# Low halves of split weights: a transfer that adds, in place of a subtraction on VectorE

## The chip, the cores and the metric

The kernel runs on one core of a Trainium2 chip. Its time is the device time of one execution in microseconds; the runs of the kernel before took 1648.26 to 1648.99 us, median 1648.5 us. Four engines compute beside each other, each with its own instruction queue worked off in order: PE (TensorE, matmuls), ACT (ScalarE), DVE (VectorE) and POOL (GpSimd). SP (SyncE) only issues transfers here.

## The reference

Two transformer blocks are computed one after the other, in fp32, for one sequence of 512 tokens with 1024 channels. The first has a gated convolution, block attention over 8 heads, cross-attention to 256 memory tokens, a gated merge and a feed-forward part of width 2816. The second has a pooling mixer, a spatial gating unit, a feed-forward part of the same width, and a gated addition. Most of the work is products with weight matrices, 151 MB in all, each weight used once:

```
proj = rmsnorm(x, g_mix) @ w_in
x = x + merged @ w_o
a, b = split(rmsnorm(x, g_ffn) @ w_up, 2)
x = x + (silu(causal_dwconv3(a)) * b) @ w_down
```

## The kernel before

All weights lie in one stream of 288 chunks, in the order in which they are used, each of 128 partitions x 1024 fp32 values (512 KB). The class `Weights` (lines 52 to 109) brings them in. `load` (line 67) issues one transfer for each chunk from SP into a raw tile `wraw`, of which there are three buffers. `make` (line 79) splits a chunk in two: ACT writes the high part `whi`, the weight rounded to the short matmul format fp32r (line 96), and DVE writes the low part `wlo`, the weight minus the high part (line 97). `whi` and `wlo` have three buffers each. The last 8 chunks are kept in tiles of their own.

`take` (line 101) hands out the next 128 or 512 columns. With the first columns of chunk c it has loads up to chunk c+2 and splits up to chunk c+1 issued. Activations are split in the same way, and every product is the sum of three matmuls, high x high, high x low and low x high:

```
mm(ps, lhsT=wh, rhs=ah, start=(k == 0), stop=False)
mm(ps, lhsT=wh, rhs=al, start=False, stop=False)
mm(ps, lhsT=wl, rhs=ah, start=False, stop=(k == n - 1))
```

These are lines 238 to 240, for products that come out with channels on partitions (`gemm_t`); lines 250 to 252 do the same for products with tokens on partitions (`gemm_n`, four tiles of 128 tokens that take turns). Both take 24 matmuls of 512 columns for one chunk. The first 8 chunks belong to the memory's keys and values, chunks 8 to 11 to the memory queries, chunks 12 to 15 to the attention queries, two steps k of the product for each chunk.

The order of instructions on each engine comes from a planner, which works with its own costs, apart from two stretches. From the start to line 459 (the products of the chunks up to 11) SP, ACT and DVE work in the order in which the program is written; PE's order is planned. From line 962 on ACT and DVE do so again.

POOL does little: it clears some tiles (lines 555, 558, 807), masks the spatial weights (line 779), scales the four `v` tiles of the gating unit (line 849), and adds squares for the last norm (line 307).

Of the kernel before, what the change touches and what calls it, by code (L numbers as in the profile page):

```python
# [7 lines left out]
F32 = mybir.dt.float32  # L8
# [3 lines left out]
AF = mybir.ActivationFunctionType  # L12
ALU = mybir.AluOpType
# [11 lines left out]
NCHUNK = 288  # L25
# [3 lines left out]


FILL = (4, 8)

ORDER = (2, 3, 1, 0)

# [17 lines left out]
class Weights:  # L52
# [26 lines left out]
    def make(self, upto, parts=1):  # L79

        while self.made < min(upto, NCHUNK):
            c = self.made
            nc = self.nc
            self.load(c + 1)
            raw = self.raw.pop(c)
            first, pool = self.stay
            if c < first:
                hi = self.pool.tile([P, CW], F32R, tag="whi", name=f"whi{c}", bufs=3)
                lo = self.pool.tile([P, CW], F32R, tag="wlo", name=f"wlo{c}", bufs=3)
            else:  # L90
                hi = pool.tile([P, CW], F32R, tag=f"whi{c}", name=f"whi{c}")
                lo = pool.tile([P, CW], F32R, tag=f"wlo{c}", name=f"wlo{c}")
            w = CW // parts
            for q in range(parts):
                s = slice(q * w, (q + 1) * w)
                nc.scalar.activation(hi[:, s], raw[:, s], AF.Copy)  # L96
                nc.vector.tensor_tensor(lo[:, s], raw[:, s], hi[:, s].bitcast(F32), ALU.subtract)  # L97
            self.chunks[c] = (hi, lo)
            self.made += 1

# [11 lines left out]
def build(ctx: ExitStack, tc: tile.TileContext, a: dict, out: bass.AP, dbg=None):  # L112
# [317 lines left out]
    def transpose_km():  # L430
        for g in range(2):
            pt = bank(ps_t, "pt", "kmt")
            for hh in range(2):
                for i in range(2):
                    c = (2 * g + hh) * P
                    nc.tensor.transpose(pt[:, hh * M + i * P: hh * M + (i + 1) * P], km_raw[i][:, c:c + P], ident)
            split(*kmT[g], pt, V("memk_gain"))


    for k in range(KT):  # L440
        if k == FILL[0]:
            transpose_km()
# [42 lines left out]
    def qkv_steps():  # L485
        for name, col, raws in (("q", 1536, q_raw), ("k", 2048, k_raw)):
            ps = [bank() for _ in range(4)]
            yield from gemm_n_steps(ps, h, "w_in", col)
            normed_rows(list(zip(raws, ps)), 8, name, rx)
        ps = [bank() for _ in range(4)]  # L490
        yield from gemm_n_steps(ps, h, "w_in", 2560)
        for i in range(4):
            src = ps[i].rearrange("p (g s d) -> p g s d", s=2, d=64)
            dst = vs[i].rearrange("p (g s o d) -> p g s o d", s=2, o=2, d=64)
            for s_ in range(2):
                split(dst[:, :, s_, s_, :], dst[:, :, s_, 1 - s_, :], src[:, :, s_, :], rx[:, i:i + 1])
# [36 lines left out]
    filler = qkv_steps()  # L533
    for _ in range(FILL[1]):
        next(filler)
# [607 lines left out]
```

## Time and profile before

| | before |
|---|---|
| median of 3 runs | 1648.5 us |
| profiled execution, its own time | 1648.37 us |
| its span, first to last instruction | 1646.7 us |
| mean granted TensorE clock | 0.998 of 2.4 GHz |
| PE, DVE, ACT, POOL busy | 99%, 57%, 39%, 2% of the span |
| DMA queue q1 (SP's transfers) | 31.4% of 16 engines' time |

A row of the timeline gives the start and the duration of an instruction in us, then engine, line of the kernel, operation, and the tile that it writes and those that it reads. Matmuls overlap: each is shown with some 0.39 us while the next starts 0.23 us after it, so rates are read from the starts. Idle time in brackets is that of the engine before the instruction, with what ended it.

### The profile page before, as it was taken

The page shows a single profiled execution, that of the slowest core. Times are in us where ns is not written, and L with a number is a line of the kernel's source. Part 1 is how long each engine was busy: PE and PEld are TensorE (multiplying, and loading weights), DVE is VectorE, ACT ScalarE, POOL GpSimd, SP SyncE. Part 2 cuts the span into 40 slices and gives each one's busy share as a digit, 9 for nine tenths or more (in the row PEclk, how much of TensorE's full clock was granted, in tenths as well). Part 3 has the DMA queues.
Part 4 walks back from the last instruction along what each step waited for, and adds up shares of the span by engine and source line. Part 5 has one row for each costly group of instructions (what it writes and reads, how often), then busy time and mean ns, then how long its engine had stood idle before and what let it go on. Part 6 is the DMA issues. An engine that isn't in the chain of part 4 may idle for free.

```text
span 1646.7 us, 18824 instructions
## 1 busy us (share of the span) xinstructions
PE 1632.1 (99%) x7495; PEld 1345.8 (82%) x7495; DVE 941.4 (57%) x1373; ACT 645.6 (39%) x926; POOL 24.8 (2%) x34
## 2 busy tenths in 40 slices
PE   8999999999999999999999999999999999999997
PEld 6788777888888888888888888888888888888896
DVE  6676785445556655653333943554567777753355
ACT  6555554223334333332224332332344444432242
POOL 0000000000000000000000300000000000000001
PEclk9999999999999999999999999999999999999999
DMA  8322222234333333332333232323332333323231
GB/s 319 108 77 65 64 57 82 93 102 143 101 96 97 95 98 96 96 102 90 102 117 100 91 103 90 92 88 103 92 114 92 100 97 96 102 90 103 90 115 52
DMA packets 47688, 165.01 MB, mean 100 GB/s; under 512 B 5361, under 2 KB 7025, under 8 KB 47601
## 3 DMA queue, kind: packets, MB, share of 16 engines
q1 hardware_dynamic: 47024, 163.04, 31.4%
q8 instruction: 58, 0.95, 0.2%
q10 hardware_dynamic: 576, 0.79, 0.1%
q14 instruction: 30, 0.24, 0.0%
HBM read 161.71 MB, written 2.10 MB: 99 GB/s over the span
## 4 chain that ended last, share of the span: by engine, by line
PE 96%; DVE 1%; DMA 1%; ACT 1%; issue 0%; ACTq 0%; DVEq 0%
PE acc L238 27%; PE acc L239 27%; PE acc L240 27%; PE acc L252 3%; PE acc L250 2%; PE acc L251 2%; DMA wraw<-in_weights 1%; PE pat L611 1%; PE acc L960 0%; PE acc L958 0%; PE acc L959 0%; PE sg L859 0%; PE oa L626 0%; PE oa L627 0%; PE sa L585 0%; ACT whi L96 0%
## 5 line engine op out<-in xcount | busy, mean ns | idle before, releaser
L96 ACT ACTIVATE whi<-wraw 128x1024 fp32r<-128x1024 f32 (+1 forms) x289 | 305.4, 1057 | 577.8 <-PE acc L239 353.6
L97 DVE TENSOR_TENSOR wlo<-wraw,whi 128x1024 fp32r<-128x1024 f32 (+1 forms) x289 | 353.3, 1222 | 221.0 <-ACT whi L96 219.5
L238 PE MATMUL acc<-h0h,whi 128*128 128x512 f32 x156 | 62.1, 398 | 0.0
L238 PE MATMUL acc<-h7h,whi 128*128 128x512 f32 x156 | 61.3, 393 | 0.0
L238 PE MATMUL acc<-h6h,whi 128*128 128x512 f32 x156 | 61.1, 392 | 0.0
L238 PE MATMUL acc<-h5h,whi 128*128 128x512 f32 x156 | 61.1, 392 | 0.0
L238 PE MATMUL acc<-h2h,whi 128*128 128x512 f32 x156 | 61.1, 391 | 0.0
L239 PE MATMUL acc<-h0l,whi 128*128 128x512 f32 x156 | 61.1, 391 | 0.0
L238 PE MATMUL acc<-h3h,whi 128*128 128x512 f32 x156 | 61.0, 391 | 0.0
L238 PE MATMUL acc<-h1h,whi 128*128 128x512 f32 x156 | 61.0, 391 | 0.0
L238 PE MATMUL acc<-h4h,whi 128*128 128x512 f32 x156 | 61.0, 391 | 0.0
L240 PE MATMUL acc<-h2h,wlo 128*128 128x512 f32 x156 | 60.9, 391 | 0.0
L239 PE MATMUL acc<-h7l,whi 128*128 128x512 f32 x156 | 60.9, 390 | 0.0
L239 PE MATMUL acc<-h2l,whi 128*128 128x512 f32 x156 | 60.9, 390 | 0.0
L240 PE MATMUL acc<-h5h,wlo 128*128 128x512 f32 x156 | 60.9, 390 | 0.0
L239 PE MATMUL acc<-h4l,whi 128*128 128x512 f32 x156 | 60.9, 390 | 0.0
L240 PE MATMUL acc<-h0h,wlo 128*128 128x512 f32 x156 | 60.9, 390 | 0.0
L239 PE MATMUL acc<-h5l,whi 128*128 128x512 f32 x156 | 60.9, 390 | 0.0
L239 PE MATMUL acc<-h1l,whi 128*128 128x512 f32 x156 | 60.8, 390 | 0.0
L240 PE MATMUL acc<-h6h,wlo 128*128 128x512 f32 x156 | 60.8, 390 | 0.0
L239 PE MATMUL acc<-h6l,whi 128*128 128x512 f32 x156 | 60.8, 390 | 0.0
L240 PE MATMUL acc<-h7h,wlo 128*128 128x512 f32 x156 | 60.8, 390 | 0.0
(1327 smaller groups left out, 4008.2 us busy)
## 6 DMA issues: line engine op xcount, KB each, us to landing
wraw<-in_weights SPq DMA_DIRECT2D x287, 512.0 KB, 3.5
xs<-in_xT SPq DMA_DIRECT2D x4, 512.0 KB, 6.2
x<-in_x SPq DMA_DIRECT2D x4, 512.0 KB, 9.3
x<-in_xT SPq DMA_DIRECT2D x8, 256.0 KB, 5.7
out<-o SPq DMA_DIRECT2D x5, 256.0 KB, 2.1
mem<-in_mem SPq DMA_DIRECT2D x2, 512.0 KB, 7.6
wraw<-in_weights SPq DMA_DIRECT2D x2, 256.0 KB, 4.6
memT<-in_memT SPq DMA_DIRECT2D x1, 512.0 KB, 7.8
```

The source lines that it names most:

```text
L96: nc.scalar.activation(hi[:, s], raw[:, s], AF.Copy)
L97: nc.vector.tensor_tensor(lo[:, s], raw[:, s], hi[:, s].bitcast(F32), ALU.subtract)
L238: mm(ps, lhsT=wh, rhs=ah, start=(k == 0), stop=False)
L239: mm(ps, lhsT=wh, rhs=al, start=False, stop=False)
L240: mm(ps, lhsT=wl, rhs=ah, start=False, stop=(k == n - 1))
L250: mm(ps, lhsT=ah[:, t], rhs=wh, start=(k == 0), stop=False)
L251: mm(ps, lhsT=ah[:, t], rhs=wl, start=False, stop=False)
L252: mm(ps, lhsT=al[:, t], rhs=wh, start=False, stop=(k == n - 1))
L611: nc.tensor.transpose(pt[:, i * P:(i + 1) * P], probs[s_][i][:, c0:c0 + P], ident)
```

## The change

For chunks 12 to 279 the subtraction on DVE is dropped. ACT writes the low tile with the negated weight, rounded in the same way as the high part, so with the negative of the high part; then a transfer issued by POOL adds the raw tile to it inside the low tile. Both tiles lie in the core's own memory (SBUF). The transfer has to wait for ACT's second pass, and PE's matmuls with the low part, and the next load into the raw tile's buffer, have to wait for the transfer. Chunks 0 to 11 and 280 to 287 are made as before.

```diff
+ADDED = range(12, NCHUNK - 8)
...
                 nc.scalar.activation(hi[:, s], raw[:, s], AF.Copy)
-                nc.vector.tensor_tensor(lo[:, s], raw[:, s], hi[:, s].bitcast(F32), ALU.subtract)
+                if c in ADDED:
+
+                    nc.scalar.activation(lo[:, s], raw[:, s], AF.Copy, scale=-1.0)
+                    nc.gpsimd.dma_start(lo[:, s], raw[:, s], accum_op=ALU.add)
+                else:
+                    nc.vector.tensor_tensor(lo[:, s], raw[:, s], hi[:, s].bitcast(F32), ALU.subtract)
```

## Rows read from the trace of the kernel before

**Rows 1.** Busy time by engine, page part 1: us, share of the span, instructions.

```profile
PE 1632.1 (99%) x7495; PEld 1345.8 (82%) x7495; DVE 941.4 (57%) x1373; ACT 645.6 (39%) x926; POOL 24.8 (2%) x34
```

**Rows 2.** Stretches of 50 us: busy us (instructions) by engine, clock, DMA share, GB/s.

```profile
0.00:50.00 50.00, 45.78 (x189) 33.68 (x189) 31.67 (x60) 30.73 (x46) 1.09 (x8) 1.00 0.77 278
50.00:100.00 50.00, 49.93 (x237) 38.88 (x236) 36.49 (x80) 28.71 (x54) 2.38 (x6) 1.00 0.32 97
...
750.00:800.00 50.00, 50.00 (x222) 41.38 (x222) 17.01 (x18) 13.18 (x15) 0.00 (x0) 1.00 0.34 103
...
900.00:950.00 50.00, 50.00 (x222) 41.42 (x221) 47.88 (x74) 18.43 (x25) 14.58 (x10) 1.00 0.33 105
...
1250.00:1300.00 50.00, 50.00 (x222) 41.42 (x221) 36.47 (x47) 22.46 (x28) 0.00 (x0) 1.00 0.31 97
...
1600.00:1650.00 50.00, 36.57 (x241) 33.39 (x239) 27.67 (x78) 14.08 (x34) 5.28 (x7) 0.92 0.12 43
```

**Rows 3.** Timeline of PE, first feed-forward part: start us, us, what, idle time before.

```profile
604.77 0.39 PE L238 MATMUL acc<-h0h,whi 128*128 128x512 f32 x1
...
610.21 0.39 PE L238 MATMUL acc<-h0h,whi 128*128 128x512 f32 x1
```

**Rows 4.** Groups by line, 277-1577 us: busy us, mean ns | idle before.

```profile
L97 DVE TENSOR_TENSOR wlo<-wraw,whi 128x1024 fp32r<-128x1024 f32 x237 | 290.8, 1227 | 199.1 <-ACT whi L96 198.2
L96 ACT ACTIVATE whi<-wraw 128x1024 fp32r<-128x1024 f32 x238 | 252.4, 1061 | 548.0 <-PE acc L239 345.7 <-issue 171.6 <-PE acc L252 19.0
```

**Rows 5.** Timeline of ACT, the stretch of rows 3.

```profile
604.74 1.06 ACT L96 ACTIVATE whi<-wraw 128x1024 fp32r<-128x1024 f32 x1 [3.06 <-PE acc L239]
605.71 0.80 ACT L636 ACTIVATE ca<-ta,vec 128x512 f32<-128x512 f32 x1
```

**Rows 6.** Timelines of POOL, ACT, DVE and PE, 903 to 930 us.

```profile
903.91 6.90 POOL L849 TENSOR_SCALAR sv<-sv,svy 128x1024 f32<-128x1024 f32 x2 [49.79 <-issue]
...
910.85 7.07 POOL L849 TENSOR_SCALAR sv<-sv,svy 128x1024 f32<-128x1024 f32 x2
...
929.04 0.12 POOL L807 MEMSET z<- 128x32 f32 x1 [8.59 <-DVE pl L820]
...
906.72 1.05 ACT L96 ACTIVATE whi<-wraw 128x1024 fp32r<-128x1024 f32 x1
...
908.09 2.06 DVE L97 TENSOR_TENSOR wlo<-wraw,whi 128x1024 fp32r<-128x1024 f32 x1
...
916.51 0.39 PE L240 MATMUL acc<-pd4h,wlo 128*128 128x512 f32 x1
```

**Rows 7.** DMA queue; line 75's issues and landings; SP's waits (us, times, longest).

```profile
q1 hardware_dynamic: 47024, 163.04, 31.4%
...
L75 SPq DMA_DIRECT2D wraw<-in_weights x289: 327/328/486, 1.2 to 1590.2; - x145
...
DMA to landing us min/median/max: 3.3/3.5/8.8
...
SPq L75 <- DVE wlo L97: 1339.8, 261, 10.7
```

**Rows 8.** Timelines of ACT, then PE, 48 to 60 us.

```profile
51.48 1.05 ACT L96 ACTIVATE whi<-wraw 128x1024 fp32r<-128x1024 f32 x1
...
53.47 1.05 ACT L96 ACTIVATE whi<-wraw 128x1024 fp32r<-128x1024 f32 x1
55.06 1.06 ACT L96 ACTIVATE whi<-wraw 128x1024 fp32r<-128x1024 f32 x1 [0.55 <-PE acc L252]
...
49.21 1.07 PE L250 MATMUL acc<-whi,h6h 128*128 128x512 f32 x4
...
55.09 0.39 PE L251 MATMUL acc<-wlo,h0h 128*128 128x512 f32 x1
...
56.45 0.39 PE L251 MATMUL acc<-wlo,h2h 128*128 128x512 f32 x1
...
57.81 0.39 PE L251 MATMUL acc<-wlo,h4h 128*128 128x512 f32 x1
```

## Prediction

> **What bounds the kernel now.** I read the busy shares first. TensorE (PE) is busy 1632.1 of 1646.7 us, 99%; DVE is at 57%, ACT at 39%, and POOL, which will issue the new transfers, at 2% [rows 1]. Then the stretches of 50 us [rows 2]: the reader is to see that PE's count stays at 222 while DVE's busy time goes from 17.01 us over 36.47 to 47.88 us, at a granted clock of 1.00, the 2.4 GHz level. So PE doesn't feel how busy DVE is. PE's idle time lies at the two ends: 4.22 us before 50 us, and 10.1 us of the last 46.7; between 50 and 100 us it is 0.07 us. Then PE's own order in time [rows 3]: a chunk of weights begins at 604.77 and the next at 610.21, 5.44 us for 24 matmuls, 0.227 us each, with no gap. PE's column of matmuls is the bound, and work taken off DVE shortens nothing in it. The question is only whether a low part now comes too late.
>
> The profiled run took 1648.37 us, the span and 1.7 us around it. The median of the runs is 1648.5 us, so I add to 1648.4.
>
> **What changes for one chunk.** 268 of the 288 chunks (12 to 279) lose a DVE subtraction of 1227 ns (237 of them between 277 and 1577 us take 290.8 us [rows 4]). All of that lay beside PE, and is worth nothing. Added for each are an ACT pass of 1061 ns [rows 4], at a pitch of 0.97 us (604.74 to 605.71 [rows 5]), and one transfer issued by POOL, which waits for that pass. ACT's total becomes 645.6 + 268 x 0.97 = 906 us, 55% of the span: no bound by itself.
>
> The cover of this chain is the ring of three buffers. ACT begins a chunk's high part at 604.74, as PE begins the chunk two before it [rows 3, 5]. A chunk's first matmul that reads the low part is its third, 0.45 us after its first, and so comes at 604.77 + 0.45 + 2 x 5.44 = 616.10. The high part starts at 604.74, the negated copy at 605.71, and that ends at 606.77. So the time from the wait's end on POOL to the landed sum, which I call A, may be 616.10 - 606.77 = 9.33 us before PE waits.
>
> A has no row. From below: POOL's issue no shorter than SP's 0.33 us, and the transfer no shorter than the fastest load of the same 512 KB, 3.3 us: 3.6 us. From above: issue as long as POOL's longest instruction here, 3.5 us (half of 6.90 us for two [rows 6]), a typical load's 3.5 us [rows 7], three times a load's share of the 16 DMA engines (read, read, write apart), and one load in the way. That share: q1 held the engines 31.4% of 1646.7 us = 517 us for 163.04 MB, so 1.66 us for one chunk. Together 3.5 + 3.5 + 2 x 1.66 + 1.66 = 12.0 us. I take 6.0: the add reads two tiles where a load reads one, so 3.5 + 1.66 = 5.2 us, and 0.8 us for the issue, near SP's 0.33 us and above it because POOL writes more addresses. 6.0 is under 9.33, so in the steady stretches the add is hidden. The engines would hold 1.66 + 3.3 = 5.0 of 5.44 us for each chunk; that is the thinnest cover here, and it fails when the add alone needs over 5.44 - 1.66 = 3.8 us.
>
> The raw buffer is released by the add instead of by DVE, and SP's next load waits for that ([rows 7]: it waits for DVE 261 times today). It is issued some 8 us after the high part's start, lands 3.5 to 5.2 us later, and is wanted three chunks, 16.3 us, after that start: 3 us remain, and what stands behind it in SP's queue has that too. Between the adds on POOL stand few instructions (34 in all [rows 1]; those that matter are below).
>
> **Where the cover is short.** At the start. Chunks 12, 13 and 14 get their high parts late, at 51.48, 53.47 and 55.06 us, because ACT is full and its order is written out; PE reads their low parts at 55.09, 56.45 and 57.81 [rows 8]. In ACT's order the three negated copies end at 53.51 (51.48 + 0.97 + 1.06), 56.47 and 58.41 us, as each pushes the next by 0.97. The third sum lands at 58.41 + A where 57.81 is wanted: with A = 6.0, PE is 6.6 us late in all, 4.4 of it at the first. Part can be filled: at 49.21 PE ran four high-part matmuls ahead of a late low part [rows 8], and of the 18 matmuls of this tile 12 read high parts, 12 x 0.227 = 2.7 us. I take 6.6 - 2.7 = 4 us; the ends are 0 (PE's order is planned so that all is filled) and 12.6 us (A = 12, nothing filled). From there on PE has no idle time to give back, so this is added to the end.
>
> And once on POOL. Between 903.91 and 917.92 us it scales the four v tiles, 14 us of work, unhurried today. The chunk whose high part starts at 906.72 has its negated copy at 908.75 and its first low-part matmul at 916.51 [rows 6]. Its add goes out at 910.81 if two of the four stand ahead of it (lands 916.8, 0.3 us late), at 917.92 if all four do (923.9, 7.4 us late). In the same stretch POOL's memsets of z wait up to 8.59 us for a buffer that DVE frees [rows 6], and an add queued behind one waits too; DVE has some 5 subtractions fewer to do there, so I price that inside the same ends. I take 3 us, between; the ends are 0 and, with A = 9.3, 10.7 us.
>
> The sum: 1648.4 + 4 + 3 = **1655.4 us**. With A from 3.6 to 9.3 this case runs from 1650 to 1666 us.
>
> A row on the two engines that share work here: DVE's subtraction at 908.09 took 2.06 us beside POOL's scaling instead of 1.22 [rows 4, 6]. If an add's issue met the same, it could wait for one DVE instruction of 1.23 us, A would be 7.2, and the sum 1656.6. The Trainium skill (page "SBUF — State Buffer", section "Who interferes with whom") says that a DVE instruction with two SBUF inputs holds up a GpSimd instruction that reads SBUF but not one that only writes there; by that rule, issuing adds is not delayed by most of this kernel's DVE work and the sum stays. No row here shows an issue on POOL beside DVE.
>
> **Rivals.** First: the transfer is too slow for the ring everywhere. A slot's cycle is 7.0 + A us (16.32 - 9.33 = 7.0), and three chunks share it, so a chunk takes (7.0 + A) / 3 once A is over 9.33. At A = 12 that is 6.33 us, 0.89 over 5.44, for 237 chunks: +211, 1859 us. Slower adds give more; it decides from A = 9.33, or from an engine time of 3.8 us for an add. For it: both unknown prices lie in one operation of which the trace has no example, and the upper bound is past the point. Against it: the load's own rows, which leave an add 2.3 loads' worth. The Trainium skill (page "Collectives: The Full Stack", section "The bandwidth ceiling: the fold count and why AG ≠ RS ≠ AR") says that an add in the DMA engines costs its second source read and not the arithmetic, and measured 1.93 times a copy; by my estimate from that page's factor 1.93 x 1.66 = 3.2 us, so this rival would not come about. No run here shows it yet.
>
> Second, on the other side: not slower. PE's order is planned anew with the adds in it; if it puts high-part matmuls ahead at 55 us until the sums have landed, and the v scaling between adds, neither stall comes, and the time is 1648.5 us. It decides from A of about 4 (then 58.41 + 4 - 57.81 = 4.6 us, of which 2.7 are filled as above and the rest by other tiles' high parts). For it: the four matmuls at 49.21. Against: other tiles' banks come free only after ACT has emptied them, and ACT gets later.
>
> Third: faster. PE would have to lose idle time after chunk 12. Between 50 and 100 us there are 0.07 us of it and none in the middle rows [rows 2]; the end's idle time lies in chunks that keep DVE. Only a shift of the planned order could give over 0.2%, to 1645 us.
>
> **Chances.** Two local stalls, 1655.4 us: 0.44, of which 0.06 end within 3.3 us of before. Too slow for the ring: 0.36, of which 0.16 lie above A = 12. Not slower: 0.16. Faster: 0.04. About 0.2%, 3.3 us, is what a measurement can tell here. Faster 0.04; within 0.2% 0.16 + 0.06 = 0.22; slower 0.38 + 0.36 = 0.74. The range goes from 1647 us to the first rival's 1859 us, and leaves out 0.04 below and 0.16 above.
>
> **What would show it.** Right: PE's count at 222 in the stretches from 300 us on, idle time of a few us on PE between 55 and 65 us that a transfer into wlo ends, and some near 915 us; POOL's adds landing some 6 us after the negated copy; DMA share near 0.9 in steady stretches, where it was 0.3. Wrong: PE's count falling in all stretches with waits on the adds (first rival), or no idle time at 55 us (second). I would be wrong in kind if PE waited in the attention stage, where chunks last longer than 5.44 us and the cover is larger.

## The result and the profile after

The changed kernel took 1671.4 us (median of 4 runs, 1670.9 to 1677.1) against 1648.6 us for the kernel before beside it: 22.7 us more, ratio 1.0147 with a 95% interval of 1.0135 to 1.0159. That is slower, well outside what a measurement can tell. I had forecast 1655.4 us: the sign was right, the size was 6.9 us where 22.7 came.

The profiled run is the longest of the four, 1677.08 us with a span of 1675.4 us. Line numbers are now 7 higher from the split on: the negated copy is L101, the add L102, the loads are L77, the low-part matmuls L247 and L258. The busy shares, the two DMA queues, the groups of the two new operations from 277 to 1577 us, and the issues with their median time to landing come first; they answer to [rows 1, 4, 7].

```profile
PE 1643.7 (98%) x7495; PEld 1354.0 (81%) x7495; DVE 635.8 (38%) x1105; ACT 890.4 (53%) x1194; POOL 252.2 (15%) x302
...
q0 software_dynamic: 38592, 140.53, 46.1%
q1 hardware_dynamic: 47024, 163.04, 30.8%
```

```profile
L101 ACT ACTIVATE wlo<-wraw 128x1024 fp32r<-128x1024 f32 x233 | 243.1, 1043 | 25.9 <-PE acc L258 25.9
L102 POOL DMA_DIRECT2D wlo<-wraw x233 | 199.2, 856 | 1068.9 <-ACT wlo L101 1045.9 <-DMA wraw<-in_weights 11.3 <-issue 6.6
```

```profile
wraw<-in_weights SPq DMA_DIRECT2D x287, 512.0 KB, 4.7
wlo<-wraw POOLq DMA_DIRECT2D x268, 512.0 KB, 5.9
```

DVE is down by 306 us, and ACT is up by 245 where 260 were worked out. An add takes 5.9 us from issue to landing, and mostly goes out 0.29 us after the end of its negated copy. A, the time from that end to the landed sum, has a median of 6.25 us over the 268 adds, and only three are over 9.33 us. I had taken 6.0. The engine time of an add is 46.1% of 1675.4 us over 268 adds, 2.88 us, where I had 3.3 and where 3.8 was the limit.

The stretches of 50 us (us, then busy us and instructions of PE, PEld, DVE, ACT and POOL, then granted clock, DMA share and GB/s) answer to [rows 2]:

```profile
50.00:100.00 50.00, 46.89 (x218) 37.60 (x217) 24.88 (x69) 35.12 (x59) 6.96 (x8) 0.97 0.72 171
750.00:800.00 50.00, 50.00 (x222) 41.39 (x221) 6.93 (x10) 23.43 (x28) 7.67 (x9) 1.00 0.85 191
850.00:900.00 50.00, 44.01 (x187) 35.40 (x186) 4.53 (x14) 21.81 (x30) 8.09 (x11) 0.93 0.74 175
900.00:950.00 50.00, 47.65 (x204) 39.01 (x203) 31.23 (x55) 26.61 (x38) 19.79 (x17) 0.97 0.74 175
950.00:1000.00 50.00, 48.15 (x210) 39.47 (x209) 13.80 (x22) 24.82 (x30) 7.49 (x10) 0.97 0.81 181
1250.00:1300.00 50.00, 46.60 (x196) 38.41 (x197) 27.64 (x47) 31.37 (x38) 7.74 (x9) 0.93 0.77 168
```

The line at 750 us is the steady case: 222 matmuls, PE full, clock 1.00, although the DMA share went from 0.34 to 0.85. Nothing is lost there. Nearly all of the loss lies in five stretches, two of which I had named, and in each of them the clock is below 1.00 as well, which I had not priced. What PE waited for (us in all, times, longest; lines of the first 20 us left out):

```profile
PE acc L258 <- DMA wlo<-wraw: 9.1, 3, 4.0
PE acc L247 <- DMA wlo<-wraw: 4.5, 3, 2.4
PE n3b L331 <- DVE ny L293: 4.4, 1, 4.4
PE n4b L331 <- DVE ny L293: 1.4, 1, 1.4
```

These are 19.4 us in eight waits. PE's timeline shows the two longest of them and the first (start, duration, what, and in brackets the idle time before it and what ended it):

```profile
57.81 0.80 PE L258 MATMUL acc<-wlo,h0h 128*128 128x512 f32 x1 [3.11 <-DMA wlo<-wraw]
58.41 0.63 PE L259 MATMUL acc<-whi,h0l 128*128 128x512 f32 x1
58.84 0.63 PE L257 MATMUL acc<-whi,h0h 128*128 128x512 f32 x1
59.26 0.63 PE L258 MATMUL acc<-wlo,h0h 128*128 128x512 f32 x1
...
885.67 0.79 PE L258 MATMUL acc<-wlo,h4h 128*128 128x512 f32 x1 [4.04 <-DMA wlo<-wraw]
...
1253.40 1.09 PE L331 MATMUL n3b<-ident,ny 128*128 128x128 f32 x4 [4.41 <-DVE ny L293]
```

Read the starts behind the first wait: 58.41, 58.84, 59.26, so 0.43 us from one matmul to the next where it was 0.227 us [rows 3]. The granted clock is 0.5 there, the 1.2 GHz level; before the wait it was 1.00. The view by stretches gives it:

```profile
58.00:60.00 2.00, 2.00 (x5) 1.61 (x6) 1.11 (x2) 2.00 (x5) 0.00 (x0) 0.50 1.16 201
```

In this run it stood at 0.5 for 23.9 us behind five of the eight waits (the last microseconds of the kernel, where the kernel before has the same, left out). 4.0 us of that lie inside waits; the other 19.9 us are work at about half speed, which loses some 10.0 us. So 19.4 + 10.0 = 29.4 us, against a difference of the two profiled runs of 28.7 us; before 20 us the changed kernel waited 1.3 us less. To within some 2 us the loss is accounted for: waits, and the clock behind them.

Where the unforeseen ones come from, one by one (the smallest, 0.31 us at 390 us, left out):

- **885 us (and 866 us), the v product.** It takes tokens on partitions, and PE runs one tile of tokens over three chunks while the other three banks wait for ACT. For that tile a chunk's cover is a few matmuls, not two chunks. The third chunk's negated copy ended at 878.44 us, and PE came to its low part at 880.93, 2.5 us later. Its add is the row below; it landed at 885.63, and PE went on at 885.67. At 866 us the cover was the usual one (855.42 to 864.50, 9.1 us), but the add itself was slow, 10.85 us, beside two 512 KB loads (`bb` and `ws`) that were issued in the same microsecond. That these loads slowed it is not shown.

```profile
878.73 0.84 POOL L102 DMA_DIRECT2D wlo<-wraw  x1 [4.58 <-ACT wlo L101]
```

- **975 us.** An add that took 7.36 us instead of 5.9, 44 us after the stall at the v scaling. Its A of 7.65 us is still under 9.33; the cover was short as well, 5.8 us from the end of its negated copy at 967.33 to PE's first idle moment at 973.17, where two products take turns on PE.
- **1253 us, the norm between the blocks.** PE waits for none of its adds. What is late is another load. The next rows are SP's issues, then ACT:

```profile
1207.00 33.70 SPq L77 DMA_DIRECT2D wraw<-in_weights  x7
1240.76 0.93 SPq L900 DMA_DIRECT2D pr<-in_pT  x2
```

```profile
1239.91 0.71 ACT L228 ACTIVATE h7h<-x,vec 128x512 fp32r<-128x512 f32 x1
1247.18 0.63 ACT L225 ACTIVATE pT0h<-pr 128x512 fp32r<-128x512 f32 x1 [6.56 <-DMA pr<-in_pT]
```

The two loads of `pr` stand in SP's queue behind a weight load that waits for a raw buffer, and that buffer is now given back by an add, which was issued at 1234.34 us and landed at 1240.32. ACT's order is written out by the planner, so ACT waits 6.56 us for `pr`; DVE's next two instructions wait for ACT, until 1249.97 us; and the norm's reduction, whose input PE had transposed from 1242.90 us on, stands behind them on DVE and runs at 1250.58. In the kernel before the same loads went out at 1214.37 us and had landed by 1219.22, as ACT came to them:

```profile
1214.37 0.91 SPq L893 DMA_DIRECT2D pr<-in_pT  x2
...
1219.19 0.62 ACT L218 ACTIVATE pT0h<-pr 128x512 fp32r<-128x512 f32 x1
```

- **1619 us, the last norm.** ACT waits for the loads of the last chunks (2.83 us at 1611.89, 1.21 us at 1615.14), DVE waits for ACT (1.96 and 0.61 us) in the middle of its chain for the norm, and that chain ends later by it.

### The profile page after: what moved, and what is told of

Read it like the earlier page. It is cut to its first block, busy times and chain, and to the rows that moved or that the text cites. A ratio compares the mean times of both kernels' runs of the same rounds, so it can differ in the third digit from the quotient of the medians.

```text
span 1675.4 us, 19518 instructions
## 1 busy us (share of the span) xinstructions
PE 1643.7 (98%) x7495; PEld 1354.0 (81%) x7495; DVE 635.8 (38%) x1105; ACT 890.4 (53%) x1194; POOL 252.2 (15%) x302
## 3 DMA queue, kind: packets, MB, share of 16 engines
q0 software_dynamic: 38592, 140.53, 46.1%
## 4 chain that ended last, share of the span: by engine, by line
PE 88%; DMA 6%; issue 2%; DVE 2%; ACT 2%; POOL 1%; ACTq 0%; DVEq 0%; POOLq 0%; SPq 0%
PE acc L247 25%; PE acc L245 25%; PE acc L246 25%; DMA wlo<-wraw 3%; DMA wraw<-in_weights 2%; PE acc L258 2%; PE acc L259 2%; PE acc L257 2%; DVE wlo L104 1%; PE pat L618 1%; DMA pr<-in_pT 0%; PE acc L967 0%; PE acc L966 0%; PE acc L965 0%; ACT whi L98 0%
## 5 line engine op out<-in xcount | busy, mean ns | idle before, releaser
L102 POOL DMA_DIRECT2D wlo<-wraw x268 | 229.3, 856 | 1335.8 <-ACT wlo L101 1243.2
L101 ACT ACTIVATE wlo<-wraw 128x1024 fp32r<-128x1024 f32 x268 | 280.0, 1045 | 31.3 <-PE acc L258 31.0
L717 DVE TENSOR_TENSOR x<-acc,x 128x512 f32<-128x512 f32 x32 | 22.1, 692 | 217.4 <-PE acc L247 217.4
L752 ACT ACTIVATE ca<-ca 128x512 f32<-128x512 f32 x44 | 27.8, 632 | 68.0 <-DVE ca L645 68.0
L247 PE MATMUL acc<-h0h,wlo 128*128 128x512 f32 x156 | 61.2, 392 | 1.9 <-DMA wlo<-wraw 1.9
L247 PE MATMUL acc<-h5h,wlo 128*128 128x512 f32 x156 | 61.0, 391 | 0.0
L246 PE MATMUL acc<-h3l,whi 128*128 128x512 f32 x156 | 61.0, 391 | 0.0
L247 PE MATMUL acc<-h1h,wlo 128*128 128x512 f32 x156 | 61.0, 391 | 0.0
L247 PE MATMUL acc<-h2h,wlo 128*128 128x512 f32 x156 | 61.0, 391 | 0.0
L247 PE MATMUL acc<-h4h,wlo 128*128 128x512 f32 x156 | 60.9, 390 | 0.0
```

The source lines that it names most:

```text
L101: nc.scalar.activation(lo[:, s], raw[:, s], AF.Copy, scale=-1.0)
L102: nc.gpsimd.dma_start(lo[:, s], raw[:, s], accum_op=ALU.add)
L717: nc.vector.tensor_tensor(x[m], add, x[m], ALU.add)
L752: nc.scalar.activation(ca, ca, func)
```

## The experiments

The theory after the result: the steady adds cost nothing; the 22.7 us are a handful of separate places where the cover is short, each with its own cause, and each wait costs more than its length because the clock falls behind it. The rival: the traffic of the adds (268 transfers, 46% of the DMA engines' time) slows the kernel as such, and the waits only show where that surfaces.

**One place at a time.** In the first kernel chunks 12 to 19 keep DVE, in the second the block with the `pr` loads stands ahead of the product before the norm, in the third DVE scales the v tiles:

```
-ADDED = range(12, NCHUNK - 8)
+ADDED = range(20, NCHUNK - 8)
```

```
+    (loads and copies of pr, pT0, pT1)
     n3 = Norm("n3")
     project(merged, "w_out_2", n3, "ffn_norm_2")
     ...
-    (loads and copies of pr, pT0, pT1)
```

```
-        nc.gpsimd.tensor_scalar(v[i], v[i], rv[:, i:i + 1], None, ALU.mult)
+        nc.vector.tensor_scalar(v[i], v[i], rv[:, i:i + 1], None, ALU.mult)
```

> The adds begin with chunk 20 instead of 12; chunks 12 to 19 keep DVE's subtraction. Theory (single stalls of PE, each with a stretch at the low clock behind it): PE's wait of 3.11 us at 57.81 and the low clock behind it, 3.08 us at half speed or 1.5 us, go: 4.6 us less than the changed kernel's 1671.4, so 1666.8 us, and no gap of PE before 300 us. Rival (the cost is spread over all adds, 22.7 us / 268 = 0.085 us each): 8 adds fewer, 0.7 us, 1670.7 us. Rival (the ring of three buffers only moves the stall to the first chunk that is added): a gap of some 3 us near 110 us, 1671 us.

> The two loads of pT and their splits are written ahead of the product with w_out_2 instead of behind it, nothing else differs from the changed kernel. Theory (SP's queue: the loads of pT stood behind a weight load that waits for an add, landed at 1249.3, and held up ACT's and DVE's order, so the norm came 4.4 us late): PE's gap of 4.41 us at 1253 goes and with it 5.6 us at half clock, 2.8 us: 1671.4 - 7.2 = 1664.2 us. Rival (DVE's chain of the norm is late for another reason, such as ACT's additional pass): the gap stays, 1671.4 us.

> The four v tiles are scaled by DVE instead of POOL (line 856), nothing else differs from the changed kernel. Theory (POOL's queue: an add whose negated copy ended at 920.12 went out at 926.97, behind scalings of 3.2 us each): PE's gap of 2.35 us at 931.5 goes, and the low clock behind it, 3.2 us at half speed or 1.6 us: 1671.4 - 4.0 = 1667.4 us, and every add goes out within 1 us of its negated copy in that stretch. Rival (the add is slow there for want of DMA bandwidth, not for POOL): gap and time stay, 1671.4 us.

Measured: 1666.4, 1667.7 and 1663.4 us; against the kernel before 1.0110 (1.0095 to 1.0125), 1.0112 (1.0093 to 1.0130) and 1.0092 (1.0077 to 1.0107), where the whole change has 1.0147. So they give back 5.0, 3.7 and 8.0 us; the ratios' intervals are each some 5 us wide, so I estimate that each of these is known to about 3 us. In the first the wait at 58 us is gone; those at 931, 975 and 1253 us stand, but the two of the v product have shrunk from 6.0 to 2.2 us and that of the last norm is gone, which the edit does not explain. In the second the wait at the norm is gone, but 2.1 us of it come back at 1195 us, where PE now waits for ACT's `m7h`, whose place in ACT's order had moved. In the third the wait at 931 us is gone and so are those at 866 and 975 us and at the last norm, which I had not expected of it; what is left of the long waits in the third:

```profile
PE acc L258 <- DMA wlo<-wraw: 7.0, 4, 3.1
PE n3b L331 <- DVE ny L293: 4.3, 1, 4.3
...
PE acc L247 <- DMA wlo<-wraw: 0.6, 1, 0.6
```

**The three together.**

> The changed kernel with three of the causes taken away where they arise and the adds kept on 260 chunks: no adds before chunk 20, the v tiles scaled by DVE instead of POOL, and the pT block (its loads and copies) put ahead of the last product before the third norm. Theory (the stalls are separate places whose prices add up): single gains 5.0, 8.0 and 3.7 us from 1671.4 give 1654.7 us; left are the stalls inside the v products (about 3 us of gap near 885 us, with half-speed work behind it) and at the last norm. Rival (the transfers' traffic as such makes the kernel some per cent slower and the stalls only move): not under 1660 us.

Measured: 1657.5 us (1656.3 to 1662.2), ratio 1.0064 (1.0049 to 1.0079): 13.9 us given back of the 16.7 that the single gains add up to, with 260 adds kept. The traffic rival's limit of 1660 us is broken by the median and by three of the four runs; the interval, 1656 to 1661 us, just takes it in. What remains is, in its profile (the longest of its runs):

```profile
PE acc L258 <- DMA wlo<-wraw: 5.1, 2, 3.4
PE acc L245 <- ACT m7h L225: 2.1, 1, 2.1
...
PE acc L247 <- DMA wlo<-wraw: 1.8, 2, 1.6
...
PE n4b L331 <- DVE ny L293: 1.2, 1, 1.2
```

That is the v product, the ACT wait that moving the block had made, the late add near 964 us, and the last norm.

**All the places at once, the steady adds kept.** DVE makes the low parts of chunks 12 to 17, 58 to 64, 144 to 168, 207 to 219 and 272 to 279; the other 209 of the 268 stay adds.

```
+ADDED = [c for c in range(18, 272) if not (58 <= c < 65 or 144 <= c < 169 or 207 <= c < 220)]
```

> DVE's subtraction is put back for 59 of the 268 chunks, those used where PE has a gap: 12 to 17, 58 to 64, 144 to 168, 207 to 219 and 272 to 279; 209 chunks still come by ACT and a transfer. Theory (steady stretches are free, all cost is in single stalls): no gap of PE behind 20 us but at the end, no stretch at the low clock, 1648.5 to 1651 us. Rival (each add costs PE something, through memory traffic or the clock): 22.7 x 209 / 268 = 17.7 us stay, 1666 us.

Measured: 1646.9 us (10 runs, 1646.5 to 1648.2), against 1648.2 for the kernel before in the same session (13 runs): ratio 0.9994, 0.9985 to 1.0004. No difference can be told. In its stretches PE is full in all the places that had lost time, also at 1250 us, where the DMA share is 0.77 with the adds on:

```profile
850.00:900.00 50.00, 50.00 (x225) 41.17 (x224) 15.89 (x31) 21.70 (x37) 1.20 (x1) 1.00 0.31 98
900.00:950.00 50.00, 50.00 (x223) 41.37 (x222) 47.93 (x70) 18.70 (x24) 14.56 (x10) 1.00 0.33 101
1250.00:1300.00 50.00, 50.00 (x223) 41.38 (x222) 26.59 (x38) 30.48 (x38) 7.64 (x9) 1.00 0.77 171
```

So 209 adds cost nothing, and nothing is gained by them either: PE's column of matmuls is the bound in both, and 239 us less of DVE work buy nothing. This is the fastest version with adds; it does not beat the kernel before by anything that can be measured.

**The traffic without anyone who needs it.** In the kernel before, POOL issues for the same chunks an add of the raw tile to itself after DVE has subtracted; nobody reads the sum.

```
                 nc.vector.tensor_tensor(lo[:, s], raw[:, s], hi[:, s].bitcast(F32), ALU.subtract)
+                if c in ADDED:
+                    nc.gpsimd.dma_start(raw[:, s], raw[:, s], accum_op=ALU.add)
```

> The kernel before, with a transfer more for chunks 12 to 279: after DVE's subtraction POOL adds the raw tile to itself, which nobody reads. So the traffic of the adds and SP's wait for them are there, but PE waits for no add and ACT has no second pass. Theory (PE's waits for late low parts and the queues make the cost, not the traffic): no gap at 55, 866, 886, 931 and 975 us; the one of the norm near 1250 us may stay, since SP's loads wait for adds here too (0 to 7.2 us): 1649 to 1656 us. Rival (traffic slows PE or lowers its clock): about the changed kernel's time, 1671 us, with the clock falling in stretches without a gap.

Measured: 1665.4 us (1660.1 to 1670.6), ratio 1.0113 (1.0096 to 1.0130). My figure was missed, and the rival's came closer. But its profile, that of the fastest of its four runs, does not show a general slowing: the stretch from 750 to 800 us has its 222 matmuls at clock 1.00 and a DMA share of 0.83, and PE has three waits over 0.25 us behind the start, none on an add. What the slower three runs lost beyond that no trace shows.

```profile
PE qmt L505 <- DVE qmr L420: 3.4, 1, 3.4
PE n3b L328 <- DVE ny L290: 3.4, 1, 3.4
PE acc L242 <- ACT pd7h L222: 3.0, 1, 3.0
```

Followed back in ACT's timeline, each begins with a load that comes late, in ACT's written order:

```profile
65.28 1.06 ACT L98 ACTIVATE whi<-wraw 128x1024 fp32r<-128x1024 f32 x1 [4.13 <-DMA wraw<-in_weights]
...
930.57 1.06 ACT L98 ACTIVATE whi<-wraw 128x1024 fp32r<-128x1024 f32 x1 [6.48 <-DMA wraw<-in_weights]
...
1233.36 0.63 ACT L222 ACTIVATE pT0h<-pr 128x512 fp32r<-128x512 f32 x1 [5.78 <-DMA pr<-in_pT]
```

The add keeps the raw buffer until it has landed, 8.7 us (median) after the start of the high part where the changed kernel has 8.3, since it begins after DVE; so the weight loads are late where the cover is short, and the `pr` loads behind them go out at 1227.91 us instead of 1214.37. This is the half of the change that I had passed over: not the sum's reader waits, but the buffer's next user, and what queues behind that on SP. This kernel cannot separate the held buffer from mere traffic, since its add holds the buffer; an add that holds nothing was not run. That the traffic alone is harmless rests on the kernel with 209 adds, and so on the steady stretches only.

**Two halves.** Each chunk is copied and added in two halves of 512 columns.

```
+            if c in ADDED:
+                parts = 2
             w = CW // parts
```

> Each chunk of the changed kernel is split in two halves of 512 columns: high part, negated copy and add for each half. The first half's low part is ready sooner (half the pass, half the transfer), traffic is the same, ACT and POOL have twice the instructions. Theory (latency of the add at the places without cover makes the stalls): the gaps at 57.8, 885.7 and 975 us shrink by some 2 us each and those of 1.9 us or less go with their low clock, about 1671.4 - 10 = 1661 us; steady stretches unchanged. Rival (DMA bandwidth makes the adds late): no gain or a loss from more descriptors, 1671 to 1680 us.

Measured: 1664.8 us, ratio 1.0100 (1.0085 to 1.0115), where I had expected about 1661. The first half lands sooner; the wait at 58 us shrinks from 3.11 to 1.47 us in two pieces, that at 931 from 2.35 to 1.25 and that at the norm from 4.41 to 2.12, and that at 975 us is gone. At 885 us it does not help: 1.10, 2.76 and 0.15 us make 4.0, as before. A shorter A helps at most places and cures one.

**A longer chain on every chunk.** Two more adds of zeros, 16 columns each, behind each add; each waits for the one before.

```
                     nc.gpsimd.dma_start(lo[:, s], raw[:, s], accum_op=ALU.add)
+                    for _ in range(2):
+                        nc.gpsimd.dma_start(lo[:, :16], self.zero[:, :16], accum_op=ALU.add)
```

> Behind each add two small adds of zeros to 16 columns of the low tile, one after the other, so that the low part is ready some 2 x 2.3 us later with hardly more traffic; the result is the same. The prediction's law of the ring: a chunk takes (7.0 + A) / 3 us once A, from the negated copy to the landed sum, is over 9.33. A was 0.3 + 5.9 = 6.2 us; with 4.6 more 10.8, so 5.93 us for a chunk instead of 5.44, 0.49 x 237 = 116 us more, plus the single stalls grown by some 4.6 us each (8 of them, 37 us): about 1671 + 150 = 1820 us, PE waiting for most chunks. Rival (the ring has more cover than I worked out, as ACT starts earlier): steady stretches stay at 5.44 us, only the single stalls grow, 1700 to 1710 us.

Measured: 2089.8 us. Now the first rival of the prediction comes about: PE waits on the chain in every stretch of 200 us from 200 us on.

```profile
PE acc L251 <- DMA wlo<-spaces: 255.5, 201, 5.7
```

I had put A at 10.8 us, so 2.3 us for each small add with its issue; it measured 13.1 (median). The two small adds landed 3.4 and 2.4 us after their issue, and part of A is POOL's queue: the large add stood there behind a small add of the chunk before. It waited for its negated copy in 87 of 268 cases only:

```profile
POOL wlo L102 <- ACT wlo L101: 57.8, 87, 3.2
```

With 13.1 the law gives (7.0 + 13.1) / 3 = 6.7 us for one chunk; the median from one negated copy to the next is 6.41 us. But POOL's own chain from the large add's landing over the two small ones takes 3.74 + 2.67 = 6.41 us by its medians, so the pitch may be set by POOL's queue, and A stretched by it. The run shows that the ring stalls everywhere once A is well over 9.33; whether a chunk then takes (7.0 + A) / 3 it cannot show. The clock was 0.952 on average, which lengthens the time further.

**What a wait costs.** The last question is whether the clock is a cost of its own. The kernel before, with the longer chain on 20 single chunks in steady stretches and DVE on all others; two small adds in one kernel, four in the other.

```
+ADDED = [*range(66, 139, 8), *range(178, 207, 8), *range(228, 269, 8)]
```

> The kernel before with 20 single stalls: in steady stretches (chunks 66 to 138, 178 to 202 and 228 to 268, every eighth) the low part comes by the negated copy and the add, with two further small adds of zeros behind it in a chain; all other chunks keep DVE's subtraction. With 11.5 to 13 us from the end of the negated copy to the last landing (as in the kernel with such a chain on every chunk) against 9.33 us of cover, PE should wait 2 to 4 us at each of the 20, 45 to 75 us in all by its own trace. Theory (the clock falls behind a gap and half-speed work adds to it): the profiled time exceeds the time before by the sum of PE's gaps and 1.5 to 3 us more at each gap, so by 30 to 60 us beyond the sum; about 1740 us. Rival (a stall costs its length, and what looked like clock was something else): the excess over the sum of the gaps is under 5 us; about 1708 us.

> The same 20 chunks with four small adds in the chain, so each gap some 6 to 7 us longer than with two: 170 to 210 us of gaps in all. Theory: the excess over the sum of the gaps is again 1.5 to 3.5 us a gap (30 to 70 us), no larger in proportion to the gap's length; about 1880 us. Rival: time = before + sum of the gaps, about 1840 us.

Measured: 1722.6 us (ratio 1.0453, 1.0430 to 1.0476) and 1789.0 us (1.0851, 1.0833 to 1.0869). The first kernel's waits in all, and one of them with what follows; then the second's:

```profile
PE acc L251 <- DMA wlo<-spaces: 48.4, 19, 3.6
```

```profile
609.58 0.76 PE L251 MATMUL acc<-h0h,wlo 128*128 128x512 f32 x1 [3.62 <-DMA wlo<-spaces]
610.14 0.63 PE L249 MATMUL acc<-h1h,whi 128*128 128x512 f32 x1
610.57 0.63 PE L250 MATMUL acc<-h1l,whi 128*128 128x512 f32 x1
```

```profile
PE acc L251 <- DMA wlo<-spaces: 86.3, 20, 6.1
```

The spans are 75.9 and 141.3 us longer than the 1646.7 us of the kernel before. The waits from 20 us on make 48.4 and 89.0 us (in the second 2.8 us of them on ACT and DVE). The excess is 27.5 and 52.3 us, so a wait does not cost its length alone: the rival, under 5 us, is out. The clock stood at 0.5 for 51.2 and 119.5 us, of which 46.9 and 96.6 us were work; half of that, 23.5 and 48.3 us, makes up nearly all of the excess. Of the 4.0 us that remain in each, up to 1.7 are half-speed work in the first 20 us; where the rest comes from stays open. The first kernel's share came out below the 30 to 60 us that I expected, as the clock fell behind 12 of its 19 waits only (all 19 are 1.5 to 3.6 us long); in the second it fell behind all 20 (3.5 to 6.1 us).

The times themselves were missed, 1740 and 1880 us expected. The single waits were shorter: in the first kernel A is 12.09 us (median), and 12.09 - 9.33 = 2.76 us is the median wait of PE; to the digit that is chance, as the waits differ from 1.46 to 3.62 us with their A. Read one by one, PE goes idle 9.46 to 9.51 us after the end of the negated copy in 18 of the 19 cases. So the cover of 9.33 us that I read from [rows 3, 5] is right within 0.2 us. In the second A is 17.56 us, which would make 8.2; PE's planned order put 17 matmuls of another tile ahead, 17 x 0.227 = 3.9 us, and 4.4 us remained.

## Why the prediction was wrong

**What held.** PE's column bounds the kernel and DVE's time is worth nothing: shown by the kernel with 209 adds, same time with 239 us less on DVE. The steady add is hidden, with A = 6.25 us for the 6.0 worked out from a load's rows. The engine time of an add, 2.9 us for 3.3, was held. The ring's limit of 9.33 us was confirmed to 0.2 us by single stalls; the law beyond it was not tested apart from POOL's queue. The adds' issues took 0.86 us for the 0.8, and none of the 268 over 1.2, so the 1.2 us more, for an issue that waits for a DVE instruction, did not come.

**The two stalls that I forecast came at about their size, in part by luck.** At the start PE waited 3.11 us, and work at half clock behind it lost 1.5: 4.6 for the 4 in the sum, and 5.0 us were given back when it was taken away. But the sum had the third low part as the latest, an A of 6.0 and 2.7 us filled by other matmuls. PE waited for the first alone, whose A was 4.88, and ran one matmul ahead; without the clock, which the sum did not have, the wait is 3.1. At the v scaling it waited 2.35 us and lost 1.6 behind it: 4.0 for 3. The add in question had its negated copy at 920.12 us and went out behind two scalings that began after it; the sum had two or four scalings ahead of an add, and 3 us as a choice between. POOL's timeline:

```profile
920.53 6.49 POOL L856 TENSOR_SCALAR sv<-sv,svy 128x1024 f32<-128x1024 f32 x2
926.97 0.88 POOL L102 DMA_DIRECT2D wlo<-wraw  x1
```

**The step that failed is the sum itself**: "1648.4 + 4 + 3" held two places where the kernel has seven with waits over 1 us, and no term for the clock. Of the 29.4 us in the profiled run, 8.6 fall to the two named places and their clock. Three things had been left out.

The first is the sentence on the raw buffer, "3 us remain, and what stands behind it in SP's queue has that too". It is true of the weight loads in the steady stages, and I left it there. What stands behind them includes two loads that ACT reaches with half a microsecond to spare; the prediction has no row on when the kernel before issues its other loads, nor on who waits for them. In place of nothing for them the run shows 4.41 us of waiting at 1253 us and 2.8 us lost by half-speed work behind it; the kernel with the block moved gave back 3.7 of it net.

The second is the cover itself. I worked it out for products with channels on partitions, two chunks ahead, and used it for all 268. In the v product PE runs one tile over three chunks, and the cover is what that tile leaves, 2.5 us: 4.04 us of waiting at 885 us. An A of 6 us is under 9.33 but not under that. At 975 us the cover was 5.8 us and the wait 1.85. The 1.95 us at 866 are another matter: there the cover was 9.1 us, and a single A was 11.15. The last norm, 1.36 us, comes by late loads, as the norm between the blocks does.

The third is the clock. I wrote that PE would be late by the length of a wait. In the profiled run 19.4 us of waits brought 10.0 us of half-speed work, and the two kernels with 20 single stalls show the same: 0.49 and 0.54 us of it for each us of waiting. With this ratio the forecast's 7 us would have been 10.5, and still short by half: places missed weigh more than the clock.

**My other statements.** That DMA share would be near 0.9 in steady stretches: it is 0.83 to 0.87. That I would be wrong in kind if PE waited in the attention stage: it did not, there is no wait over 0.25 us between 58 and 390 us, and 0.31 us at 390.35. "Not slower" fell with the first wait. "Too slow for the ring" did not come about; with A made 13.1 us PE waited in all stages, though POOL's queue had a part in that.

**What stays open.** Moving the v scaling to DVE also took away the waits at 866 and 975 us, 8.0 us in all where 4.0 was its own place, and leaving out the first eight adds shrank waits at 866 and 885 us that lie 800 us behind them. The planner orders each kernel anew, so the single kernels differ in more than their edit; I did not separate these, and the single gains are to be read with that. Nor do the runs say why kernels with such waits vary by 3 to 11 us from run to run, where the kernel before varies by 0.7 to 2.3 and the one with 209 adds by 1.7; in their profiles the clock falls behind some waits and not behind others of the same length.

## What to carry to other kernels

When an operation gets longer but is covered in the steady state, list every place where the cover is not the steady one: other loop orders, the ends of stages, and each instruction that shares a queue with the one that now waits for a buffer. A buffer that is given back later moves all that stands behind its next load, also loads of other data that had just been in time. And price a wait of the engine at the bound at about one and a half times its length here, since the clock fell to half behind most of them.

## What the runs showed of the hardware that I had not expected

- The granted clock fell to 0.5 behind waits as short as 1.75 us, with 0.31 more right behind, on an engine that had been full for tens of us (in the kernel with the moved block, at 1195 us), though not behind all: in the two kernels with single stalls, 12 of 19 waits of 1.5 to 3.6 us, and all 20 of 3.5 to 6.1 us.
- An add of 512 KB inside SBUF takes 4.4 us from issue to landing when it runs alone among loads (20 of them, loads at 3.5 us), and 5.9 us when there is one for each chunk (loads then at 4.7). It held the 16 engines 2.88 us where a load of the same size held them 1.66, so 1.74 times as long.
- The size matters little at the short end: in the two kernels with single stalls an add of 8 KB took 4.8 us (median) to land where it followed a large add, and 2.0 to 2.9 us further down the chain, against 4.4 us for 512 KB. A chain of small transfers pays that for each, as each waits for the one before.
